# One transformer layer on one core: operand tiles alike modulo 512 bytes, border sums on VectorE, border loads ahead of the output product

## The chip, the cores and the metric

The kernel runs on 1 core of one Trainium2 chip. The metric is the device time of one execution in microseconds (us); lower is better. Each time is the median of several executions, with the lowest and the highest beside it. A profile is one execution of its own, with its own time.

## The reference

One layer over 2048 tokens of width 1024, with 256 context tokens, all in float32. The first half ends in the merge, the second is the feed-forward part:

```
y = sigmoid(ga) * (attn_o @ w_br_attn) + sigmoid(gb) * (gm_o @ w_br_gm)   # 512 -> 1024, twice
x = x + g1 * (y @ w_out)                                                  # 1024 -> 1024
h = rmsnorm(x, g) * (1 + scale) + shift
x = x + g2 * (square(relu(h @ w_ff1)) @ w_ff2)                            # 1024 -> 4096 -> 1024
```

Ahead of it stand the modulated norm, one input projection, attention (8 heads over 2 key heads, with rotary positions) and a gated branch over 128-token chunks.

## The kernel before

**Precision.** Each float32 operand of a large product is split into a high part (a rounding cast, mostly on ScalarE, lines L144, L970, L1139, L1174, L1180) and a low part (the difference, on VectorE or GpSimd, L148, L971, L1140, L1175, L1181). A product is then three matmuls (high x high, high x low, low x high): `mm3` (L176 to L178) in the merge, `product` (L1211 to L1213) in the feed-forward part. One matmul takes a 128x128 stationary tile and a 128x512 moving tile.

**Stages.** Projection, attention, merge (1479 to 1858 us in the trace), then feed-forward 1 and 2 for the first half of the tokens (to 2167 and 2480) and for the second (to 2800 and 3139). The merge takes four token blocks `b` of 512. In each, 8 steps `m` multiply the branch outputs (tiles `in`, moving) with the branch weights (`bw`, stationary), 24 matmuls a step; the gates `gt` multiply the sums, and the result is split into `y`. Then the output product follows: 4 row groups `tt` of two halves `n`, 24 matmuls each (`y` stationary, `wo` moving); VectorE multiplies each half with the gate (`jk`, L953) and a sum adds it to the residual `xt` (L955), which is stored (L957) and squared for the norm (L960). The branch weights are fetched and split anew in every block.

**Feed-forward 1** replaces eight block products by seven (a Strassen-like scheme over the two halves of the tokens and of the width). Group by group (`ff1_group`), the seven products of four 128-row steps each use sums of the normed input (`he` or `hl` tiles, high and low, moving) and of the weights (`f4`, `f2`, or `f8` for the first group, stationary). `f8` tiles hold loaded rows of x or weights, `f2` tiles sums and results in float32.

**The border.** What the first group needs is made during the output product of the last block (`b` = 3) by the generator `h_early`, which `merge` steps with `next(side)` after each half. For each of four inputs `kk` it loads x (`h_fetch`, L985, four transfers), scales it (`h_scaled`, L992), transposes it in four banks of four 128x128 blocks (`h_turn`, L182), moves them out through ScalarE (L999), and `combine` forms the sums; `halves` splits them. `h_last` forms one more sum; `h_rest`, stepped in the first group, splits what is left. `w1_fetch` loads the first group's weights (L1121), `w1_plain` and `w1_combine` make their parts and sums, and `w1_ops` the remaining parts, in steps.

**Order and memory.** Each engine runs its own queue in a fixed order, which a scheduler sets from the program's order and the dependencies; the method `order` keeps each tag's tiles in the order in which the program makes them. Tiles lie in pools on a left and a right side of the on-chip memory. The pool `edge` with the one tile `pd` is opened on the right first; so the right-hand tiles below it (`in`, `raw`, then `f8`, `f2`, `he`) start at addresses that its size shifts: 448 bytes past a multiple of 512 with `pd` of 8 floats. The left-hand tiles (`y`, `wo`, `bw`, `hl`, `f4`) start at multiples of 512.

```
self.open("edge", side="right")
self.nc.gpsimd.memset(self.sb("pd", [8]), 0.0)
self.open("pre", side="right")
```

Of the kernel before, what the change touches and what calls it, by code (L numbers as in the profile page):

```python
# [10 lines left out]
F32R = mybir.dt.float32r  # L11
I32 = mybir.dt.int32
AF = mybir.ActivationFunctionType
ALU = mybir.AluOpType
# [53 lines left out]
class Kern:  # L68
# [809 lines left out]
    def merge(self, first, start, last):  # L878
        nc = self.nc
        for _ in start:  # L880
            pass
        self.close("mid", "base")
        self.open("out")
        self.open("branch")
        steps = [(b, m) for b in range(NB) for m in range(KC)]
        it = iter(steps)
        q = []
        w_out = self.load_w_out()

        def fetch(lo_eng="pool"):  # L890
            s = next(it, None)
            if s is not None:
                q.append((self.br_weights(self.br_raw(s[1]), lo_eng), self.gate_in(*s)))

        inp = first
        early = [(s, self.br_raw(s[1])) for s in (next(it), next(it))]
        for s, raw in early:
            q.append((self.br_weights(raw, "dve"), self.gate_in(*s)))
        for b in range(NB):
            y = []  # L900
            for m in range(KC):
# [11 lines left out]
                nc.vector.tensor_tensor(out=gt["a"], in0=gt["a"], in1=gt["g"], op=ALU.add)  # L913
                yh, yl = self.sb("y", [TB], F32R), self.sb("y", [TB], F32R)
                self.split(gt["a"], yh, yl)
                y.append((yh, yl))
                if b == 0:
                    next(w_out, None)
                    if m == 2:
                        last.sums(self.sb("raw", [TB]))  # L920
                    if m == 4:
                        last.inverse()
            inp = {}
            if b + 1 < NB:
                side = self.br_inputs(b + 1, inp)
            else:
                self.close("branch", "pre")
                self.open("early", side="right")
                side = self.h_early()
            for tt in range(TT):  # L930
                tok = slice(tt * P, (tt + 1) * P)
                xt = self.sb("xt", [D])
                nc.sync.dma_start(xt, self.x_block(b)[tok, :])
                banks = [self.bank([512]) for _ in range(2)]

                def outer(n, ks):
                    cs = slice(n * 512, (n + 1) * 512)
                    for k in ks:
                        self.mm3(
                            banks[n], y[k][0][:, tok], y[k][1][:, tok], self.wo[k][0][:, cs],  # L940
                            self.wo[k][1][:, cs], k == 0, k == KC - 1,
                        )

                head = KC - 1 if tt == 0 else KC
                if tt == 0:
                    for n in range(2):
                        outer(n, range(head))
                for n in range(2):
                    cs = slice(n * 512, (n + 1) * 512)
# [3 lines left out]
                    nc.vector.tensor_tensor(out=part, in0=ps, in1=self.g1b[:, cs], op=ALU.mult)  # L953
                    eng = nc.vector if b + 1 < NB or tt + 1 == TT else nc.gpsimd
                    eng.tensor_tensor(out=xt[:, cs], in0=xt[:, cs], in1=part, op=ALU.add)  # L955
                    next(side, None)
                nc.sync.dma_start(self.x1_d[b][tok, :], xt)  # L957
# [75 lines left out]
    def h_early(self):  # L1033
        nc = self.nc
        add, sub = ALU.add, ALU.subtract
        self.h0 = h = [[None] * (KC // 2) for _ in range(7)]
        self.h0_src = src = {}

        def tt(out, in0, in1, op):
            nc.vector.tensor_tensor(out=out, in0=in0, in1=in1, op=op)  # L1040

        def ptt(out, in0, in1, op):
            nc.gpsimd.tensor_tensor(out=out, in0=in0, in1=in1, op=op)

        def done(kk, *ps):
            for p in ps:
                h[p][kk] = self.halves(kk, p, src[kk, p])

        def turn(kk, j):
            for i in range(2):  # L1050
                raw[kk, i, j] = self.h_turn(x[kk], kk, i, j)

        def combine(kk, tt):
# [12 lines left out]
        for kk in range(3):  # L1066
            x[kk] = self.h_fetch(0, kk)
        yield
        self.h_scaled(x[0], rb)
        turn(0, 0)  # L1070
        yield
        turn(0, 1)
        self.h_scaled(x[1], rb)
        combine(0, tt)
        done(0, 5)
        yield
        x[3] = self.h_fetch(0, 3)
        turn(1, 0)
        self.h_last(0, tt)
        done(0, 1, 6, 4)  # L1080
        yield
        turn(1, 1)
        self.h_scaled(x[2], rb)
        done(0, 3, 2)
        yield
        raw1 = self.w1_fetch(0)
        turn(2, 0)
        combine(1, tt)
        yield
        turn(2, 1)  # L1090
        self.h_scaled(x[3], rb)
        combine(2, ptt)
        yield
        turn(3, 0)
        turn(3, 1)
        combine(3, ptt)
        self.w1_first = self.w1_early(raw1)
        yield

    def h_last(self, kk, tt):  # L1100
        s2 = self.h0_src[kk, 2] = self.h0_src[kk, 5]
        tt(s2, self.h0_src[kk, 1], s2, ALU.subtract)

    def h_rest(self):
        h, src = self.h0, self.h0_src
        nc = self.nc

        def ptt(out, in0, in1, op):
            nc.gpsimd.tensor_tensor(out=out, in0=in0, in1=in1, op=op)

        for p in (5, 1, 6, 4, 3, 2):
            for kk in range(1, KC // 2):
                h[p][kk] = self.halves(kk, p, src[kk, p])
                if p == 5:
                    self.h_last(kk, ptt)
            yield

    def w1_fetch(self, g):
# [18 lines left out]
    def w1_plain(self, raw, hr, lr, out):  # L1137
# [8 lines left out]
    def w1_early(self, raw):  # L1146
        out = {}
        hl = self.sb("f8", [2, KC, P], F32R)
        self.w1_plain(raw, hl[:, 0], hl[:, 1], out)
        t = self.sb("f8", [2, 2, KC // 2, P])  # L1150
        self.w1_combine(raw, t[:, 0], t[:, 1])
        return out, raw, t[:, 0], t[:, 1]

    def w1_ops(self, g, out):
        if g == 0 and self.w1_first:
# [116 lines left out]
    def ff1(self, blk, h, extra):  # L1272
# [1 line left out]
        first = self.w1_ops(0, w[0])  # L1274
        rest = iter(()) if blk else self.h_rest()
        if blk == 0:
            for it in (first, rest, rest, first, first):
                next(it)
        for _ in first:
            pass  # L1280
        for g in range(NG):
            nxt = iter(())
            if g + 1 < NG:
# [2 lines left out]
            else:  # L1286
                self.ready = [self.ff2_chunk(blk, 0, 0)]
            more = extra(g)
            for _ in self.ff1_group(blk, g, w.pop(g), h):
                next(rest, None)  # L1290
                next(nxt, None)
                next(more, None)
            for _ in nxt:
# [111 lines left out]
    def build(self):  # L1405
# [312 lines left out]
```

## Time and profile before

| | |
|---|---|
| time, median of 3 (lowest to highest) | 3144.84 us (3142.81 to 3146.82) |
| profiled execution, its own time | 3140.78 us |
| its span in the trace | 3139.0 us |
| mean granted TensorE clock | 0.99 of full |
| busy: PE, DVE, ACT, POOL | 3066.5, 1947.1, 1352.2, 942.8 us |
| merge, border and first feed-forward group | 1479 to 1900 us of the span |

The profiled execution lies 4.06 us under the median, and 1.78 us of it lie outside the span. In the profile's rows PE is TensorE, PEld its weight loads, DVE VectorE, ACT ScalarE, POOL GpSimd and SP the engine whose queue issues the transfers. A row of a timeline gives the start and the duration in us, then engine, line, operation, output tile<-input tiles (`f` stands for f2, f4 and f8, `b` for a bank of the accumulation memory), and in brackets how long the engine had been idle and what ended that. Matmuls are pipelined: a record lasts longer than the distance to the next one's start.

### The profile page before, as it was taken

Reading aid. Unit: us, or ns where it says so; the run is one execution under the profiler, and the core shown is the slowest. Engines: PE = TensorE matmul, PEld = TensorE weight load, DVE = VectorE, ACT = ScalarE, POOL = GpSimd, SP = SyncE. Lnnn points to the kernel's source line nnn. Section 1 sums busy time; section 2 is a strip of 40 time slices with the busy share of each in tenths; the row PEclk is TensorE's granted clock in tenths of the full one; section 3 lists DMA queues with packets and bytes.
Section 4 is the critical chain, followed back from the end, with each engine's and each line's share of the span. In section 5 each row is a group of like instructions: output and inputs, shape, how many; then the busy total and the mean of one; then the engine's idle time right before and its main releaser. Section 6 shows DMA issues by size and latency. Waiting matters only on the chain.

```text
span 3139.0 us, 38055 instructions
## 1 busy us (share of the span) xinstructions
PE 3066.5 (98%) x13892; PEld 2305.2 (73%) x13892; DVE 1947.1 (62%) x2782; ACT 1352.2 (43%) x2058; POOL 942.8 (30%) x650
## 2 busy tenths in 40 slices
PE   8999999999999999999999999999999999999999
PEld 4888788877655555555777877888777788888777
DVE  4735666466677777667643478876654676654445
ACT  3353434333455555554322244444543344444433
POOL 1423323241688888887143230000000000000000
PEclk9999999999999999999999999999999999999999
DMA  6354655535100000003855548888576644445665
GB/s 202 110 181 118 203 156 179 185 98 174 38 14 4 21 8 18 11 8 93 270 159 162 158 138 313 307 298 279 196 256 205 212 146 152 153 144 194 207 214 201
DMA packets 332174, 485.42 MB, mean 155 GB/s; under 512 B 33969, under 2 KB 166321, under 8 KB 331986
## 3 DMA queue, kind: packets, MB, share of 16 engines
q1 hardware_dynamic: 324002, 478.38, 46.0%
q10 hardware_dynamic: 7984, 4.61, 0.5%
q8 instruction: 109, 1.79, 0.2%
q14 instruction: 79, 0.65, 0.1%
HBM read 348.56 MB, written 134.35 MB: 154 GB/s over the span
## 4 chain that ended last, share of the span: by engine, by line
PE 80%; DVE 7%; DMA 5%; POOL 3%; issue 2%; ACT 2%; SPq 0%; ACTq 0%; POOLq 0%; DVEq 0%
PE b L1212 12%; PE b L1213 12%; PE b L1211 11%; PE b L1610 8%; PE b L176 8%; PE b L178 8%; PE b L177 8%; PE b L1577 5%; PE b L1596 4%; PE b L1542 3%; PE b L182 2%; DMA bw<-in_w_br_gm 1%; DMA f<-w2o_d 1%; DMA w<-in_w_in 1%; POOL bw L148 1%
## 5 line engine op out<-in xcount | busy, mean ns | idle before, releaser
L1305 DVE TENSOR_TENSOR f<-f,f 128x1024 fp32r<-128x1024 f32 x224 | 273.1, 1224 | 267.4 <-ACT f L1304 264.2
L1553 DVE TENSOR_REDUCE ts<-b 128x1 f32<-128x512 f32 x512 | 314.8, 683 | 172.3 <-PE b L1542 172.3
L1304 ACT CAST f<-f 128x1024 fp32r<-128x1024 f32 x224 | 235.3, 1053 | 332.1 <-DMA f<-ao_d 289.6
L1212 PE MATMUL b<-f,f 128*128 128x512 f32 x896 | 350.9, 392 | 5.3 <-DVE f L1305 4.6
L1213 PE MATMUL b<-f,f 128*128 128x512 f32 x896 | 348.9, 389 | 0.0
L1626 POOL TENSOR_TENSOR ac<-ac,p 128x512 f32<-128x512 f32 x216 | 296.7, 1407 | 70.4 <-ACT p L1600 69.4
L1211 PE MATMUL b<-f,f 128*128 128x512 f32 x896 | 306.8, 392 | 11.0 <-ACT b L1347 4.9
L1600 ACT ACTIVATE p<-b 128x512 f32<-128x512 f32 x384 | 199.6, 614 | 158.0 <-PE b L1596 154.8
L148 POOL TENSOR_TENSOR w<-w,w 128x1024 fp32r<-128x1024 f32 x60 | 146.6, 2444 | 400.9 <-ACT w L144 166.7
L1626 POOL TENSOR_TENSOR ac<-ac,t 128x512 f32<-128x512 f32 x160 | 232.1, 1477 | 3.1 <-ACT t L1600 3.1
L1212 PE MATMUL b<-hl,f 128*128 128x512 f32 x576 | 226.6, 393 | 0.4 <-DVE hl L971 0.4
L1211 PE MATMUL b<-hl,f 128*128 128x512 f32 x576 | 225.8, 392 | 0.0
L1213 PE MATMUL b<-hl,f 128*128 128x512 f32 x576 | 224.5, 390 | 0.0
L144 ACT CAST w<-w 128x1024 fp32r<-128x1024 f32 x120 | 125.9, 1049 | 219.0 <-DMA w<-in_w_in 188.9
L176 PE MATMUL b<-t,w 128*128 128x512 f32 x512 | 204.9, 400 | 4.6 <-DVE t L590 4.2
L1211 PEld LDWEIGHTS b<-f,f 128*128 128x128 f32 x896 | 167.4, 188 | 52.1 <-ACT f L1304 8.2
L1212 PEld LDWEIGHTS b<-f,f 128*128 128x128 f32 x896 | 168.2, 188 | 46.6 <-DVE f L1305 12.2
L177 PE MATMUL b<-t,w 128*128 128x512 f32 x512 | 201.2, 393 | 0.0
L178 PE MATMUL b<-t,w 128*128 128x512 f32 x512 | 201.2, 393 | 0.0
L1577 PE MATMUL b<-t,t 128*128 128x512 f32 x576 | 198.1, 414 | 2.9 <-ACT p L1600 2.7
L178 PE MATMUL b<-w,t 128*128 128x512 f32 (+1 forms) x528 | 192.0, 364 | 2.6 <-POOL t L148 2.5
L1213 PEld LDWEIGHTS b<-f,f 128*128 128x128 f32 x896 | 168.2, 188 | 34.5
(230 smaller groups left out, 6518.5 us busy)
## 6 DMA issues: line engine op xcount, KB each, us to landing
w<-in_w_in SPq DMA_DIRECT2D x120, 512.0 KB
ao_d<-f SPq DMA_DIRECT2D x224, 256.0 KB
f<-ao_d SPq DMA_DIRECT2D x112, 512.0 KB
f<-w2o_d SPq DMA_DIRECT2D x112, 512.0 KB
f<-in_w_ff SPq DMA_DIRECT2D x48, 1024.0 KB
w2o_d<-f SPq DMA_DIRECT2D x112, 256.0 KB
md<-in_w_mod SPq DMA_DIRECT2D x32, 512.0 KB
f<-x_d SPq DMA_DIRECT2D x64, 256.0 KB
```

The source lines that it names most:

```text
L176: mm(ps, sh, mh, start=start, stop=False)
L177: mm(ps, sh, ml, start=False, stop=False)
L178: mm(ps, sl, mh, start=False, stop=stop)
L1211: mm(ps, wh, hh, start=start and k == 0, stop=False, skip_group_check=True)
L1212: mm(ps, wh, hl, start=False, stop=False, skip_group_check=True)
L1213: mm(ps, wl, hh, start=False, stop=k == len(w) - 1, skip_group_check=True)
L1304: nc.scalar.copy(h, f32(l))
L1305: nc.vector.tensor_tensor(out=l, in0=f32(l), in1=f32(h), op=ALU.subtract)
L1553: nc.vector.tensor_reduce(out=self.mx[:, t, h, c : c + 1], in_=ps[h], axis=AX.X, op=ALU.max)
L1577: self.nc.tensor.matmul(self.pts[j][h], k.KA[c][self.kv][:, ks], self.qa[h], start=True, stop=False, skip_group_check=True,)
L1610: nc.tensor.matmul(self.o[h * HD : (h + 1) * HD, :], k.V[c][:, i, self.kv * HD : (self.kv + 1) * HD], pt[h], start=j == 0, stop=j == NKT - 1,)
L1626: nc.gpsimd.tensor_tensor(out=self.acc[e][:, h], in0=old[:, h], in1=pt[h], op=ALU.add)
```

## The change

1. `pd` has 120 floats instead of 8 (480 bytes instead of 32), which shifts all right-hand tiles by 448 bytes, to multiples of 512.
2. Fifteen sums at the border go from GpSimd to VectorE: six into `xt`, six of `combine` (for `kk` = 2 and 3) and three of `h_last`.
3. `h_early` is cut anew. Its first step (the loads for `kk` = 0 to 2) is taken ahead of the output product; each later step transposes a whole input (16 blocks); the first group's weights are loaded a step earlier; and the last step of `w1_ops` (the split for product 2) goes behind the fourth product of the first group instead of ahead of the first.

```diff
@@ merge
                 side = self.h_early()
+                next(side)
...
-                    eng = nc.vector if b + 1 < NB or tt + 1 == TT else nc.gpsimd
-                    eng.tensor_tensor(out=xt[:, cs], in0=xt[:, cs], in1=part, op=ALU.add)
+                    nc.vector.tensor_tensor(out=xt[:, cs], in0=xt[:, cs], in1=part, op=ALU.add)
                     next(side, None)
@@ h_early
-        def turn(kk, j):
-            for i in range(2):
-                raw[kk, i, j] = self.h_turn(x[kk], kk, i, j)
+        def turn(kk):
+            self.h_scaled(x[kk], rb)
+            for j in range(2):
+                for i in range(2):
+                    raw[kk, i, j] = self.h_turn(x[kk], kk, i, j)
...
         yield
-        self.h_scaled(x[0], rb)
-        turn(0, 0)
-        yield
-        turn(0, 1)
-        self.h_scaled(x[1], rb)
-        combine(0, tt)
+        turn(0)
+        yield
+        combine(0)
         done(0, 5)
-        yield
         x[3] = self.h_fetch(0, 3)
-        turn(1, 0)
-        self.h_last(0, tt)
-        done(0, 1, 6, 4)
-        yield
-        turn(1, 1)
-        self.h_scaled(x[2], rb)
-        done(0, 3, 2)
-        yield
+        yield
+        turn(1)
         raw1 = self.w1_fetch(0)
-        turn(2, 0)
-        combine(1, tt)
-        yield
-        turn(2, 1)
-        self.h_scaled(x[3], rb)
-        combine(2, ptt)
-        yield
-        turn(3, 0)
-        turn(3, 1)
-        combine(3, ptt)
-        self.w1_first = self.w1_early(raw1)
-        yield
+        self.h_last(0)
+        done(0, 1, 6)
+        yield
+        done(0, 4, 3, 2)
+        combine(1)
+        yield
+        turn(2)
+        combine(2)
+        yield
+        turn(3)
+        out, hl = {}, self.sb("f8", [2, KC, P], F32R)
+        self.w1_plain(raw1, hl[:, 0], hl[:, 1], out)
+        yield
+        combine(3)
+        t = self.sb("f8", [2, 2, KC // 2, P])
+        self.w1_combine(raw1, t[:, 0], t[:, 1])
+        self.w1_first = out, raw1, t[:, 0], t[:, 1]
+        yield
@@ h_rest
-                    self.h_last(kk, ptt)
+                    self.h_last(kk)
@@ ff1
-            for it in (first, rest, rest, first, first):
+            for it in (first, rest, rest, first):
                 next(it)
-        for _ in first:
-            pass
+        else:
+            for _ in first:
+                pass
...
-            for _ in self.ff1_group(blk, g, w.pop(g), h):
+            for n, _ in enumerate(self.ff1_group(blk, g, w.pop(g), h)):
                 next(rest, None)
+                if n == 3:
+                    next(first, None)
@@ build
-        self.nc.gpsimd.memset(self.sb("pd", [8]), 0.0)
+        self.nc.gpsimd.memset(self.sb("pd", [120]), 0.0)
```

The queues change only at the border. First, TensorE's queue before, at the end of the output product (`wo`, `y`), where the fourth input's transposes (L182, `ident`; x4 is four blocks in one bank) stand between it and the first product of feed-forward 1 (L1211):

```order
L176 MATMUL b_15978<-wo_13560,y_15628 128x512
L177 MATMUL b_15978<-wo_13561,y_15628 128x512
L178 MATMUL b_15978<-wo_13560,y_15629 128x512
L182 MATMUL b_16056<-ident,f_3566_15832 128x128 x4
L182 MATMUL b_16063<-ident,f_3566_15832 128x128 x4
L182 MATMUL b_16070<-ident,f_3566_15832 128x128 x4
L182 MATMUL b_16077<-ident,f_3566_15832 128x128 x4
L1211 MATMUL b_16145<-he_15796,f_3623_16092 128x512
L1212 MATMUL b_16145<-he_15797,f_3623_16092 128x512
```

Now, TensorE's queue has the same four rows of transposes ahead of the last row group of the output product:

```order
L176 MATMUL b_15902<-wo_13560,y_15628 128x512
L177 MATMUL b_15902<-wo_13561,y_15628 128x512
L178 MATMUL b_15902<-wo_13560,y_15629 128x512
L182 MATMUL b_15995<-ident,f_3560_15770 128x128 x4
L182 MATMUL b_16002<-ident,f_3560_15770 128x128 x4
L182 MATMUL b_16009<-ident,f_3560_15770 128x128 x4
L182 MATMUL b_16016<-ident,f_3560_15770 128x128 x4
L176 MATMUL b_16031<-wo_13164,y_15317 128x512
L177 MATMUL b_16031<-wo_13165,y_15317 128x512
```

Behind them 48 output matmuls follow, and then the first product, whose line is now L1195 (L1211 to L1213 became L1195 to L1197).

Second, ScalarE's queue at the start of feed-forward 1, before: the split of product 2's weights (L1180), the weight casts (L1174), the casts of the inputs, and last the copy of the first product's bank (L1230):

```order
L960 ACTIVATE jk_3625_16100,ss2_78<-xt_3600_15975 128x1024
L1180 CAST f2_3642_16141<-f8_3591_15948 128x512
L1174 CAST f4_3626_16106<-f8_3624_16095 128x1024
L970 CAST hl_3628_16110<-f2_3568_15842 128x512
L1174 CAST f4_3640_16137<-f8_3624_16095 128x1024
L970 CAST hl_3630_16115<-f2_3593_15955 128x512
L970 CAST hl_3632_16120<-f2_3613_16061 128x512
L970 CAST hl_3634_16125<-f2_3583_15903 128x512
L970 CAST hl_3636_16129<-f2_3605_16011 128x512
L970 CAST hl_3638_16133<-f2_3617_16075 128x512
L1230 COPY f2_3646_16159<-b_3644_16145 128x512
```

Now the same place of ScalarE's queue (L1214 is the copy, L1158 the weight cast):

```order
L960 ACTIVATE jk_3625_16100,ss2_78<-xt_3616_16029 128x1024
L1214 COPY f2_3644_16155<-b_3642_16141 128x512
L1158 CAST f4_3626_16106<-f8_3623_16068 128x1024
L970 CAST hl_3628_16110<-f2_3567_15815 128x512
L1158 CAST f4_3640_16137<-f8_3623_16068 128x1024
L970 CAST hl_3630_16115<-f2_3595_15936 128x512
L970 CAST hl_3632_16120<-f2_3607_16000 128x512
L970 CAST hl_3634_16125<-f2_3571_15829 128x512
L970 CAST hl_3636_16129<-f2_3599_15950 128x512
L970 CAST hl_3638_16133<-f2_3611_16014 128x512
```

The copy moved from behind the casts to ahead of them, and the split L1180 went from this place to a later one.

Third, VectorE's queue at the same place, now (L1159 is the low part of the weights, before L1175; L1097 is `h_last`, before L1109 on GpSimd):

```order
L955 TENSOR_TENSOR xt_16029<-xt_16029,jk_16096 128x512
L1159 TENSOR_TENSOR f_3627_16107<-f_3623_16068,f_3626_16106 128x1024
L971 TENSOR_TENSOR hl_16111<-f_3567_15815,hl_16110 128x512
L1159 TENSOR_TENSOR f_3641_16138<-f_3623_16068,f_3640_16137 128x1024
L1097 TENSOR_TENSOR f_3567_15815<-f_3571_15829,f_3567_15815 128x512
L971 TENSOR_TENSOR hl_16116<-f_3595_15936,hl_16115 128x512
L971 TENSOR_TENSOR hl_16121<-f_3607_16000,hl_16120 128x512
L1097 TENSOR_TENSOR f_3595_15936<-f_3599_15950,f_3595_15936 128x512
L1097 TENSOR_TENSOR f_3607_16000<-f_3611_16014,f_3607_16000 128x512
L971 TENSOR_TENSOR hl_16126<-f_3571_15829,hl_16125 128x512
```

The three rows of L1097 are new in this queue; the sums of `combine` (L1040) and into `xt` (L955) stand ahead of these rows. GpSimd's queue ends with the last split of `y` in the merge.

More of the change, by code (lines that the diff above doesn't have):

```diff
@@ L1040, in tt @@
             nc.vector.tensor_tensor(out=out, in0=in0, in1=in1, op=op)
-        def ptt(out, in0, in1, op):
-            nc.gpsimd.tensor_tensor(out=out, in0=in0, in1=in1, op=op)
         def done(kk, *ps):
@@ L1047, in done, with combine @@
                 h[p][kk] = self.halves(kk, p, src[kk, p])
-        def turn(kk, j):
-            for i in range(2):
-                raw[kk, i, j] = self.h_turn(x[kk], kk, i, j)
-        def combine(kk, tt):
+        def turn(kk):
[3 more added lines that the diff above has]
+                    raw[kk, i, j] = self.h_turn(x[kk], kk, i, j)
+        def combine(kk):
             r = {(i, j): raw[kk, i, j] for i in range(2) for j in range(2)}
@@ L1068, in h_early, with h_last @@
         yield
-        self.h_scaled(x[0], rb)
-        turn(0, 0)
+        turn(0)
         yield
-        turn(0, 1)
-        self.h_scaled(x[1], rb)
-        combine(0, tt)
+        combine(0)
         done(0, 5)
+        x[3] = self.h_fetch(0, 3)
         yield
-        x[3] = self.h_fetch(0, 3)
-        turn(1, 0)
-        self.h_last(0, tt)
-        done(0, 1, 6, 4)
+        turn(1)
+        raw1 = self.w1_fetch(0)
+        self.h_last(0)
+        done(0, 1, 6)
         yield
-        turn(1, 1)
-        self.h_scaled(x[2], rb)
-        done(0, 3, 2)
+        done(0, 4, 3, 2)
+        combine(1)
         yield
-        raw1 = self.w1_fetch(0)
-        turn(2, 0)
-        combine(1, tt)
+        turn(2)
+        combine(2)
         yield
-        turn(2, 1)
-        self.h_scaled(x[3], rb)
-        combine(2, ptt)
+        turn(3)
+        out, hl = {}, self.sb("f8", [2, KC, P], F32R)
+        self.w1_plain(raw1, hl[:, 0], hl[:, 1], out)
         yield
-        turn(3, 0)
-        turn(3, 1)
-        combine(3, ptt)
-        self.w1_first = self.w1_early(raw1)
+        combine(3)
+        t = self.sb("f8", [2, 2, KC // 2, P])
+        self.w1_combine(raw1, t[:, 0], t[:, 1])
+        self.w1_first = out, raw1, t[:, 0], t[:, 1]
         yield
-    def h_last(self, kk, tt):
+    def h_last(self, kk):
         s2 = self.h0_src[kk, 2] = self.h0_src[kk, 5]
-        tt(s2, self.h0_src[kk, 1], s2, ALU.subtract)
+        self.nc.vector.tensor_tensor(
+            out=s2, in0=self.h0_src[kk, 1], in1=s2, op=ALU.subtract
+        )
     def h_rest(self):
         h, src = self.h0, self.h0_src
-        nc = self.nc
-        def ptt(out, in0, in1, op):
-            nc.gpsimd.tensor_tensor(out=out, in0=in0, in1=in1, op=op)
         for p in (5, 1, 6, 4, 3, 2):
@@ L1144, in w1_plain @@
         out[1] = [(hr[:, H + k, :], lr[:, H + k, :]) for k in range(H)]
[L1146 to L1152, printed above, removed]
     def w1_ops(self, g, out):
```

## Prediction

> **What bounds the kernel now.** I read the busy times first, then the chain, then stretches of one stage at a time.
>
> ```profile
> span 3139.0 us, 38055 instructions
> PE 3066.5 (98%) x13892; PEld 2305.2 (73%) x13892; DVE 1947.1 (62%) x2782; ACT 1352.2 (43%) x2058; POOL 942.8 (30%) x650
> PE 80%; DVE 7%; DMA 5%; POOL 3%; issue 2%; ACT 2%; SPq 0%; ACTq 0%; POOLq 0%; DVEq 0%
> ```
>
> TensorE carries 80% of the chain, so two things can move the end: the pitch of its matmuls, and its pauses. The windows on PE alone show the pitch (us, busy time, number, granted clock, DMA share, GB/s); in each PE is busy throughout at full clock.
>
> ```profile
> core 0: us, PE busy (x), PEclk, DMA share, GB/s
> 1534.00:1564.00 30.00, 30.00 (x134) 1.00 0.77 257
> 1770.00:1800.00 30.00, 30.00 (x130) 1.00 0.50 149
> 1900.00:2160.00 260.00, 260.00 (x1130) 1.00 0.89 306
> 2920.00:2950.00 30.00, 30.00 (x134) 1.00 0.57 191
> ```
>
> A matmul reaches 0.39 us past its start, so a 30 us window holds starts over 30.39 us. The first (output product, `wo` and `y`) gives 30.39/134 = 226.8 ns, the second (branch product, `in` and `bw`) 30.39/130 = 233.8 ns, the third (feed-forward 1, mostly `he` or `hl` against `f`) 260.39/1130 = 230.4 ns, the last (feed-forward 2) 226.8 ns. All are 128x512 float32 products. By tile, the third window splits:
>
> ```profile
> 1900.00:2160.00 260.00, 105.64 (x399) 74.76 (x400) 0.00 (x0) 0.00 (x0) 1.00 0.89 306
> 1900.00:2160.00 260.00, 180.37 (x731) 136.64 (x729) 0.00 (x0) 0.00 (x0) 1.00 0.89 306
> 2565.95 0.39 PE L1211 MATMUL b<-he,f 128*128 128x512 f32 x1
> 2569.44 0.39 PE L1211 MATMUL b<-hl,f 128*128 128x512 f32 x1
> ```
>
> The first row is `he` (399 matmuls), the second `hl` (731). The last two bracket an unbroken run of 15 `he` products: 3.49/15 = 232.7 ns. Then `hl` costs (260.39 - 399 x 0.2327)/731 = 229.2 ns. So the operands that start 448 bytes past a multiple of 512 (`in`, `he`) stream at 233 ns against a weight tile at 0, and those at 0 against 0 (`wo`, `y`, `hl`) at 227 to 229. A busy PE hides this, since overlapping records fill the window either way.
>
> **The change, part by part.**
>
> *Alignment.* The larger `pd` shifts every right-hand tile by 448 bytes, so `in`, `raw`, `f8`, `f2` and `he` come to 0 modulo 512, as the left-hand tiles are. The counts, from the groups by tile (duration min/median/max, first and last start):
>
> ```profile
> L1211 PE MATMUL b<-he,f x320: 389/394/796, 1857.9 to 2814.9; 128*128 128x512 f32 x160
> L176 PE MATMUL b<-in,bw x256: 392/394/628, 1479.2 to 1806.6; 128*128 128x512 f32 x128
> ```
>
> The other two lines of each product have as many: 960 `he` and 768 `in` matmuls. For `he` I take the pitch of `hl`, its neighbour in the same groups: 3.5 ns x 960 = 3.4 us; with feed-forward 2's pitch it would be 5.9 ns x 960 = 5.7 us. The lower end is zero (a rival). Feed-forward 1 runs without pauses from 1900 on, so the gain reaches the end. The shifted `f2` weights have no pitch of their own in a row; I cost them at nothing, within 0.5 us.
>
> In the merge only matmuls on the path count. The chain by line for 1479 to 1858, and for the stretch in which the third token block's branch products run:
>
> ```profile
> by line: PE b L178 24.4%; PE b L176 24.2%; PE b L177 23.9%; DMA bw<-in_w_br_gm 11.4%; POOL bw L148 7.5%; issue 2.2%; ACT bw L144 2.2%; PE b L182 1.5%; POOL y L148 0.7%; DVE gt L913 0.4%; DVE in L148 0.4%; PE b L1652 0.3%; POOLq L148 0.2%; D
> by line: POOL bw L148 36.7%; DMA bw<-in_w_br_gm 35.8%; issue 8.8%; ACT bw L144 7.2%; POOL y L148 4.1%; PE b L178 3.6%; PE b L176 1.9%; PE b L177 1.9%; POOLq L148 1.1%; ACTq L144 0.1%
> ```
>
> L176 to L178 hold 72.5% of 379 us = 275 us. The output product's 768 matmuls take 768 x 0.2268 = 174 us of that, which leaves 101 us, or 430 of the 768 branch matmuls at 0.2338. The second row (1688 to 1722) says why the others don't count: weights are fetched and split there, and a faster PE only waits longer. 430 x 7.0 ns = 3.0 us; with the `he`/`hl` difference, 430 x 3.5 = 1.5. I take 2.3. Both ends: nothing, and 768 x 7.0 = 5.4.
>
> [...]
>
> *Border: adds and order.* Fifteen additions leave GpSimd for VectorE (six into `xt`, six in `combine`, three in `h_last`). VectorE does such an operation in 0.60 to 0.69 us; the rows show what it costs beside GpSimd.
>
> ```profile
> 1852.13 4.88 POOL L1043 TENSOR_TENSOR f<-f,f 128x512 f32<-128x512 f32 x3 [5.85 <-ACT f L999]
> 1866.53 2.20 POOL L1109 TENSOR_TENSOR f<-f,f 128x512 f32<-128x512 f32 x1 [1.90 <-DVE hl L971]
> 1869.36 3.35 POOL L1109 TENSOR_TENSOR f<-f,f 128x512 f32<-128x512 f32 x2 [0.63 <-DVE hl L971]
> 1860.21 1.62 DVE L971 TENSOR_TENSOR he<-f,he 128x512 fp32r<-128x512 f32 x1
> 1867.50 5.75 DVE L971 TENSOR_TENSOR hl<-f,hl 128x512 fp32r<-128x512 f32 x4
> 1873.17 0.68 DVE L1181 TENSOR_TENSOR f<-f,f 128x512 fp32r<-128x512 f32 x1
> 1850.10 0.69 DVE L953 TENSOR_TENSOR jk<-b,g 128x512 f32<-128x512 f32 x1 [1.41 <-PE b L178]
> ```
>
> Twelve of the fifteen go ahead of the first feed-forward product: 12 x 0.6 = 7.2 us of new VectorE work, hidden in its idle time of 1.41 us before the last row and like gaps from 1815 to 1858. Without that cover they cost 7.2 us. The other three, 3 x 0.6 = 1.8 us, fall in the first group, where VectorE has no room:
>
> ```profile
> 1868.00:1900.00 32.00, 28.75 (x117) 22.01 (x117) 31.96 (x44) 18.13 (x30) 4.08 (x3) 0.97 0.79 272
> 1857.91 0.48 PE L1211 MATMUL b<-he,f 128*128 128x512 f32 x1
> 1861.88 0.50 PE L1212 MATMUL b<-he,f 128*128 128x512 f32 x1 [1.15 <-DVE he L971]
> 1864.64 0.80 PE L1211 MATMUL b<-he,f 128*128 128x512 f32 x1 [2.03 <-ACT f L1174]
> 1866.92 0.63 PE L1211 MATMUL b<-he,f 128*128 128x512 f32 x1
> 1867.35 0.63 PE L1212 MATMUL b<-hl,f 128*128 128x512 f32 x1
> 1874.00 0.50 PE L1211 MATMUL b<-he,f 128*128 128x512 f32 x1 [2.34 <-ACT f L1230]
> 1888.88 0.50 PE L1213 MATMUL b<-he,f 128*128 128x512 f32 x1 [0.31 <-DVE f L1175]
> ```
>
> VectorE is busy 31.96 of 32 us, yet four subtractions of 0.6 took 5.75, beside GpSimd. PE waits 1.15, 2.03 and 2.34 us; after the second its pitch is 0.43 us instead of 0.23 (1866.92 to 1867.35) for about a dozen matmuls: 12 x 0.2 = 2.4 us at half clock. The last row is the 88th feed-forward matmul, 30.97 us after the first; 87 at 230.4 ns need 20.0, so the border now costs 11 us.
>
> After the change the fourth input's 16 transposes stand ahead of 48 output matmuls (48 x 0.2268 = 10.9 us), so its `he` is ready at the start: the first product loses nothing (gain: 1.15 us of wait). The copy of its result (0.59) now stands in ACT's queue ahead of the cast L1158 (before: L1174) of the second weights, and VectorE's subtraction L1159 behind that:
>
> ```profile
> 1863.54 1.04 ACT L1174 CAST f<-f 128x1024 fp32r<-128x1024 f32 x1 [1.81 <-DVE f L1135]
> 1864.62 1.23 DVE L1175 TENSOR_TENSOR f<-f,f 128x1024 fp32r<-128x1024 f32 x1 [1.11 <-ACT f L1174]
> 1873.36 0.59 ACT L1230 COPY f<-b 128x512 f32<-128x512 f32 x1 [4.70 <-DVE hl L971]
> ```
>
> 0.59 + 1.04 + 1.23 = 2.9 us pass between the first product's end and the second's last weights. Nine matmuls of the third product and then those of the second that need only the high part run in that time, so I see waits of about 0.8, 0.3 and 0.7 us. From there VectorE paces PE, with each low part 0.6 (an `hl`) or 1.2 us (weights) after the last, three adds between them: eight waits of 0.2 to 1.7, together some 6 us. Sum: 20.0 + 1.8 + 6 = 27.8, against 30.97: 3.2 us. Of these 2.4 are the half clock; it followed a wait of 2.03, and none of my waits is that long. They could chain, so I take 2.8; the ends are +4 and, with half clock back and 1.8 us of adds uncovered, 4.2 - 3.2 = 1.0 lost.
>
> *Moved loads.* The fourth input's four issues and the weights' one stand earlier in SP's queue, each past one store of `x1`.
>
> ```profile
> 1799.85 10.02 SPq L985 DMA_DIRECT2D f<-x_d  x12
> 1826.89 2.02 SPq L985 DMA_DIRECT2D f<-x_d  x4
> 1834.53 0.33 SPq L957 DMA_DIRECT2D x_d<-xt  x1
> 1838.29 0.37 SPq L1121 DMA_DIRECT2D f<-in_w_ff  x1
> ```
>
> SP is idle from 1828.9 to 1834.5 and nothing that PE waits for comes from those stores: nothing, unless the weights came late, and they only come earlier. The 12 early loads stood ahead of the output product already.
>
> *Sum:* 3.4 + 2.3 + 2.8 = 8.5 us. The profiled execution, 3140.78 us (its span and 1.78 outside), becomes 3132.3. The median of three lies 4.06 above it, so 3136.3.
>
> **The rivals.**
>
> 1. *Alignment pays nothing.* The 7 ns come from something else that sets these stages apart, such as which side of memory a tile is on. For it: `hl` at 0 is still 2.4 ns over feed-forward 2. Against: `in` and `he`, in stages with different DMA load (0.50 and 0.89), show the same 233. [...] Only the border's 2.8 is left: 3142.0.
> 2. *Waits take the gains back.* In the merge a PE 7 ns faster waits for the weights as in the 1688 to 1722 row, and VectorE's queue gives the border nothing. Only `he` pays: 3144.8 - 3.4 = 3141.4. DMA at 0.89 in feed-forward 1 works the same way.
> 3. *All of it pays.* 5.7 + 5.4 + 4 = 15.1: 3129.7.
> 4. *Slower: VectorE's queue at the border.* The 15 adds find no idle time, because the transposes' results and the squares in ACT's queue come later than I see; each then costs its 0.69 us on the path, 10.4 in all, and the product that waits for the last of them waits over 2 us, so that the half clock comes a second time (2.4). Against it: the idle stretches of VectorE before 1858. It decides at a wait of 2.0 us at a product behind the first. 10.4 + 2.4 - 5.7 of alignment = 7.1 lost: 3151.9.
>
> **How the numbers follow.** The forecast 0.50, its own range a gain of 5 to 12 us (3132.8 to 3139.8); rival 1 0.17; rival 2 0.14; rival 3 0.10; rival 4 0.09. A measurement here can tell 0.2% = 6.3 us from no change. The forecast falls beyond 6.3 in four fifths of its cases (0.40), rival 3 always (0.10), rival 2 in 0.04: faster 0.54 and I add 0.04 for rival 1 where the border alone gives much. Slower is two thirds of rival 4: 0.06 (the rest of it, with less than the full price, is no change). The rest, 0.36, is no change. Leaving out the far ends of rivals 3 and 4, the range is 3130 to 3144.
>
> **What would show it.** Right: the stretch of `in` holds 133 or 134 matmuls in 30 us; 260 us of feed-forward 1 hold 1134 or more; no GpSimd addition after the merge's last split; no half-clock pitch after the first feed-forward product; its 88th matmul about 28 us after it. Wrong: 130 matmuls in `in`'s stretch (rival 1), longer waits for `bw` and `y` at an unchanged merge (rival 2), or a wait over 2 us on ACT's cast in the first group (rival 4).

## The result and the profile after

| | before | after |
|---|---|---|
| time, median of 4 (lowest to highest) | 3145.60 us (3142.81 to 3146.82) | 3122.80 us (3120.28 to 3126.11) |
| profiled execution: span | 3139.0 us | 3119.3 us |

The ratio of after to before is 0.9929, with a 95% interval from 0.9912 to 0.9947: 22 us faster, between 17 and 28. The forecast was 3136.3 us, with a range from 3130 to 3144; the measured time lies under it. One execution of a kernel below, e6, took 7220.89 us at a granted clock of 0.40 and is left out of that kernel's time.

The page of after, in the same rows as before's, and the windows on PE alone (us, busy time, number of matmuls, granted clock, DMA share, GB/s):

```profile
span 3119.3 us, 38046 instructions
PE 3045.5 (98%) x13892; PEld 2299.1 (74%) x13892; DVE 1937.7 (62%) x2797; ACT 1352.0 (43%) x2058; POOL 917.5 (29%) x635
PE 79%; DVE 7%; DMA 6%; POOL 3%; ACT 2%; issue 2%; SPq 0%; ACTq 0%; DVEq 0%; POOLq 0%
...
1534.00:1564.00 30.00, 30.00 (x134) 1.00 0.64 217
1770.00:1800.00 30.00, 30.00 (x134) 1.00 0.58 180
1900.00:2140.00 240.00, 240.00 (x1059) 1.00 0.89 314
2490.00:2760.00 270.00, 270.00 (x1192) 1.00 0.41 145
```

The bound is the same engine; PE is busy throughout in each window, as before. Only the counts tell what changed. The second row's 30 us, nearly all of them branch products, hold 134 matmuls instead of 130: 30.39/134 = 226.8 ns. The first 240 us of feed-forward 1 hold 1059, 227.0 ns each. The same windows of before:

```profile
1900.00:2140.00 240.00, 240.00 (x1043) 1.00 0.89 306
2490.00:2760.00 270.00, 270.00 (x1174) 1.00 0.43 147
```

1059 against 1043 is 16 matmuls, 3.6 us in 240; that is more than `he` alone could give, as the tile rows of after show (first `he`, then `hl`, each with its number of matmuls):

```profile
1900.00:2140.00 240.00, 97.16 (x375) 69.78 (x373) 0.00 (x0) 0.00 (x0) 1.00 0.89 314
1900.00:2140.00 240.00, 167.45 (x684) 128.50 (x685) 0.00 (x0) 0.00 (x0) 1.00 0.89 314
```

(375 + 684) x 227.0 ns fill the window: if `hl` had stayed at 229.2, its 684 alone would leave 240.39 - 156.8 = 83.6 us, or 223 ns for each `he`, less than the pitch of any stage in these traces. Both went to 227.

The starts of the second half of the tokens, averaged by place in the product, say where `hl` lost. In five of the seven products of a group three `he` matmuls are followed by nine `hl`, with `f4` weights; neither `hl` nor `f4` moved. Before, the first five `hl` took 226, 236, 228, 233 and 231 ns and only those from the sixth on 227; after, all take 226 to 227. So the slow pitch of `he` ran on into its neighbours. Product 2, the last of a group, is another case: its weights are `f2` tiles, which the larger `pd` does move, from 448 to 0, so that its `hl` matmuls, at 0, stood 448 bytes off their own weights. The distance from its first row to that of the next group (two rows of before, then two of after) was 2.78 us and is 2.72:

```profile
2563.17 0.39 PE L1211 MATMUL b<-he,f 128*128 128x512 f32 x1
2565.95 0.39 PE L1211 MATMUL b<-he,f 128*128 128x512 f32 x1
2548.38 0.39 PE L1195 MATMUL b<-he,f 128*128 128x512 f32 x1
2551.10 0.39 PE L1195 MATMUL b<-he,f 128*128 128x512 f32 x1
```

Of some 327 ns lost in a group of 84 matmuls, the `he` matmuls themselves made 172, the `hl` matmuls behind them 99, and product 2 made 56.

The border, PE's waits summed for 1845 to 1905 (engine, line, what it waited for: us in total, times, longest):

```profile
PE b L1196 <- DVE hl L971: 2.1, 3, 1.1
PE b L1197 <- DVE f L1159: 1.9, 2, 1.4
PE b L1195 <- ACT f L1214: 0.7, 1, 0.7
PE b L1197 <- DVE f L1132: 0.2, 1, 0.2
```

```profile
1849.13 0.39 PE L1195 MATMUL b<-he,f 128*128 128x512 f32 x1
...
1876.87 0.50 PE L1197 MATMUL b<-he,f 128*128 128x512 f32 x1 [1.37 <-DVE f L1159]
...
1877.98 0.63 PE L1197 MATMUL b<-hl,f 128*128 128x512 f32 x1
1878.41 0.63 PE L1195 MATMUL b<-hl,f 128*128 128x512 f32 x1
```

The waits are the ones forecast: ACT's copy (0.7), the second weights (0.5 of the 1.9), then VectorE's low parts. The 88th matmul comes 27.74 us after the first (forecast 27.8, before 30.97). The half clock is back at another place, behind the last wait: pitch 0.43 us from about 1877.6 on, at a granted clock of 0.50 from 1877.50 to 1880.00, some 1.6 us lost. From the 88th to the 121st product it takes 9.23 us here, and 7.60 in the trace of e5, which has no half clock there.

Of the 19.7 us between the two spans, 6.8 lie ahead of the merge, 1.9 in it, 3.2 between the first and the 88th feed-forward product, 1.7 in the rest of feed-forward 1's first half and 4.7 in its second half; the rest lies elsewhere. The first branch product starts at 1479.2 us before and at 1472.3 after:

```profile
L176 PE MATMUL b<-in,bw x256: 387/389/500, 1472.3 to 1797.9; 128*128 128x512 f32 x128
```

Nothing is changed in the queues ahead of that point. Whether the addresses did that had to be tested.

### The profile page after: what moved, and what is told of

Its sections match the earlier page's. It is cut to its first block, busy times and chain, and to the rows that moved or that the text cites. A ratio compares the mean times of both kernels' runs of the same rounds, so it can differ in the third digit from the quotient of the medians.

```text
span 3119.3 us, 38046 instructions
## 1 busy us (share of the span) xinstructions
PE 3045.5 (98%) x13892; PEld 2299.1 (74%) x13892; DVE 1937.7 (62%) x2797; ACT 1352.0 (43%) x2058; POOL 917.5 (29%) x635
## 4 chain that ended last, share of the span: by engine, by line
PE 79%; DVE 7%; DMA 6%; POOL 3%; ACT 2%; issue 2%; SPq 0%; ACTq 0%; DVEq 0%; POOLq 0%
PE b L1196 12%; PE b L1197 12%; PE b L1195 11%; PE b L1597 8%; PE b L176 7%; PE b L178 7%; PE b L177 7%; PE b L1564 5%; PE b L1583 4%; PE b L1529 3%; PE b L182 2%; DMA bw<-in_w_br_gm 1%; DMA w<-in_w_in 1%; DVE f L1292 1%; DMA f<-ao_d 1%
## 5 line engine op out<-in xcount | busy, mean ns | idle before, releaser
L1197 PE MATMUL b<-f,f 128*128 128x512 f32 x896 | 348.9, 389 | 0.0
L1195 PE MATMUL b<-f,f 128*128 128x512 f32 x896 | 306.6, 391 | 10.2 <-ACT b L1334 4.5
L1195 PE MATMUL b<-hl,f 128*128 128x512 f32 x576 | 224.6, 390 | 0.0
L1197 PE MATMUL b<-hl,f 128*128 128x512 f32 x576 | 224.3, 390 | 0.0
L1195 PEld LDWEIGHTS b<-f,f 128*128 128x128 f32 x896 | 167.5, 188 | 50.8 <-ACT f L1291 7.0
L1197 PEld LDWEIGHTS b<-f,f 128*128 128x128 f32 x896 | 168.2, 188 | 34.4
```

The lines of the kernel that those rows point to most:

```text
L1195: mm(ps, wh, hh, start=start and k == 0, stop=False, skip_group_check=True)
L1197: mm(ps, wl, hh, start=False, stop=k == len(w) - 1, skip_group_check=True)
```

## The experiments

Theories: (A) alignment, the border and a chance difference ahead of the merge add up; (B) what is gained ahead of the merge belongs to the change; (C) order and sums bring most of it. Each timed kernel was run beside the kernel before on the same chip; ratios are to that, with a 95% interval.

**e1, no alignment** (all else changed):

```diff
-        self.nc.gpsimd.memset(self.sb("pd", [120]), 0.0)
+        self.nc.gpsimd.memset(self.sb("pd", [8]), 0.0)
```

> The changed kernel with pd at 8 floats again: sums and order as changed, right-hand tiles back at 448 modulo 512. Theory A (alignment, border and chance ahead of the merge add up): 260 us of feed-forward 1 hold about 1130 matmuls again, 30 us of the in/bw stretch 130; the 88th feed-forward product stays about 28 us after the first; time 3142 us (3139 to 3145), 3 us under before. The merge's start in the trace falls anywhere from 1472 to 1481 us. Theory B (the 6.8 us gained ahead of the merge belong to the addresses): the merge starts at 1478 or later. Theory C (order and sums bring most of the 22.8 us): 3130 or less.

Measured: 3133.63 us against 3138.94, ratio 0.9986 (0.9977 to 0.9994): 4.4 us faster (2 to 7). That is theory A's 3 us in size; the time itself lies under the expected range because the kernel before was faster too in this comparison than in the first. Feed-forward 1 is back at the pitch of before; the 88th product comes 27.30 us after the first; the merge starts at 1479.7.

```profile
1900.00:2140.00 240.00, 239.99 (x1040) 1.00 0.88 308
2490.00:2760.00 270.00, 270.00 (x1174) 1.00 0.43 149
```

**e2, alignment alone** (`pd` of 120 floats in the kernel before):

```diff
-        self.nc.gpsimd.memset(self.sb("pd", [8]), 0.0)
+        self.nc.gpsimd.memset(self.sb("pd", [120]), 0.0)
```

> The kernel before with pd at 120 floats: alignment alone. Theory A: feed-forward 1 at 227 ns a matmul for he and hl alike, 2688 x 3.5 ns = 9.4 us less, the merge 2 to 3 less, border as before (88th product some 30.5 us after the first, half clock kept): 3133.5 us (3130 to 3137). Theory B: another 6.8 us less, 3127, and the merge starts at 1473. Theory C: 3142 or more.

Measured: 3124.23 us, ratio 0.9955 (0.9943 to 0.9967): 14.1 us faster (10 to 18). Theory A expected 11 us less than before and theory B 18, and the interval holds both; the border and the merge's start tell more. The border stays as it was (30.97 us to the 88th product).

```profile
1900.00:2140.00 240.00, 240.00 (x1060) 1.00 0.87 312
2490.00:2760.00 270.00, 270.00 (x1192) 1.00 0.41 144
```

The two parts add to 18.5 us. Theory C falls. The merge started at 1478.0 us here, not near theory B's 1473, so with the new addresses too it can start as late as with the old.

**e3, the border's sums alone** (order and `pd` as before):

```diff
-                    eng = nc.vector if b + 1 < NB or tt + 1 == TT else nc.gpsimd
-                    eng.tensor_tensor(out=xt[:, cs], in0=xt[:, cs], in1=part, op=ALU.add)
+                    nc.vector.tensor_tensor(out=xt[:, cs], in0=xt[:, cs], in1=part, op=ALU.add)
...
-            nc.gpsimd.tensor_tensor(out=out, in0=in0, in1=in1, op=op)
+            nc.vector.tensor_tensor(out=out, in0=in0, in1=in1, op=op)
```

> The kernel before with the fifteen border sums on VectorE and nothing else changed (the order of loads and transposes and pd of 8 as before). If the contention with GpSimd is the border's loss, the 88th feed-forward product comes 28 us after the first and the time is 3142; if the order of the transposes is, the sums add to VectorE's queue and it comes 31 to 33 us after: 3145 to 3148.

Measured: 3136.31 us, ratio 0.9991 (0.9981 to 1.0002), 2.6 us less in the median, which this can't tell from none. But in the trace the 88th product comes 27.95 us after the first, 3.0 sooner, although half clock follows the wait of 1.5 us as it did before. No GpSimd instruction runs beside VectorE any more; VectorE's subtractions take 0.6 to 0.7 us each where four took 5.75 before, and the long wait of 2.3 us for ACT's copy is gone (three waits of PE, then a row of VectorE).

```profile
PE b L1210 <- ACT f L1173: 1.5, 1, 1.5
PE b L1211 <- DVE he L970: 0.6, 1, 0.6
PE b L1211 <- DVE hl L970: 0.4, 1, 0.4
1876.92 1.28 DVE L970 TENSOR_TENSOR hl<-f,hl 128x512 fp32r<-128x512 f32 x2
```

**e10, the new order alone, at the new addresses** (the fifteen sums on GpSimd again in the changed kernel; one execution):

```diff
-                    nc.vector.tensor_tensor(out=xt[:, cs], in0=xt[:, cs], in1=part, op=ALU.add)
+                    eng = nc.vector if b + 1 < NB or tt + 1 == TT else nc.gpsimd
+                    eng.tensor_tensor(out=xt[:, cs], in0=xt[:, cs], in1=part, op=ALU.add)
...
+            tt = ptt if kk > 1 else vtt
...
-        self.nc.vector.tensor_tensor(
+        eng = self.nc.gpsimd if kk else self.nc.vector
+        eng.tensor_tensor(
```

> The changed kernel with its new order and its addresses, but the fifteen sums on GpSimd as before. If the sums bring the border's 3 us, the 88th feed-forward product comes about 31 us after the first, or later; if the new order brings it, about 27.5.

Measured: 3126.89 us; the 88th product after 29.26 us, between the two: the order alone brings 1.7 us, the sums alone 3.0, both together 3.2 to 3.7. They overlap, and neither theory's number was met. With the sums on GpSimd the slow subtractions are back:

```profile
1865.18 5.79 DVE L972 TENSOR_TENSOR hl<-f,hl 128x512 fp32r<-128x512 f32 x4
```

What the order takes away is the wait of 1.5 to 2.0 us for the cast of the second weights: it stands in all four traces with the old order (before, e2, e3 and e6), each time with half clock behind it (a pitch of 0.43 us in before and e3), and in none with the new.

**e5, the changed kernel again**, beside e6, a kernel with alignment and sums in the old order:

> The changed kernel once more, unchanged, beside e6 on one chip. Theory A (alignment 12 to 14 us, border 3 to 4, the rest of the 22.8 us chance in the merge's start): 16 to 19 us under before. Theory B (the part ahead of the merge belongs to the change): 21 us or more under before, and the merge starts near 1472 again. A half clock behind the wait of 1.4 us at the 88th product comes in some executions and not in others.

> The kernel before with pd at 120 floats and the fifteen sums on VectorE, but with the loads, transposes and splits in the order of before. If the new order of h_early brings something, this is 1 us or more slower than the changed kernel; if the sums bring all of the border's gain, the two are equal within their scatter, 16 to 19 us under before, and the 121st feed-forward product comes 33.5 to 35.7 us after the first (changed kernel: 36.97 with a half clock).

Measured: the changed kernel 3122.89 us, ratio 0.9957 (0.9941 to 0.9973), 13.5 us faster (8 to 19); the other 3121.7 in four executions, ratio 0.9949 (0.9934 to 0.9963). They are equal within their scatter: on top of the sums, the new order brings nothing that the times can show; in the traces the 88th product comes 0.7 us sooner with it (27.27 against 27.94). Nor do the times show the border's gain on top of alignment, which alone gave 14.1 us in e2; it is seen in e1's time and in the traces. The changed kernel took the same time as in the first comparison (3122.8); it was the kernel before that read 3145.6 there, and 3138.3 here. The merge starts at 1479.4 in this trace of the changed kernel, 7 us later than in the first. Over all traces of this case it starts at 1472.3 to 1481.8 with distances that are multiples of 256 bytes (eight traces, mean 1478.7) and at 1477.1 to 1485.4 with others (six, mean 1480.1). Theory B isn't borne out; what a small mean difference there is, these traces can't tell from scatter.

The half clock behind the 88th product didn't come in e5's trace, after the same wait:

```profile
1881.17 0.50 PE L1197 MATMUL b<-he,f 128*128 128x512 f32 x1 [1.37 <-DVE f L1159]
1881.50 0.40 PE L1195 MATMUL b<-hl,f 128*128 128x512 f32 x1
1881.73 0.39 PE L1196 MATMUL b<-hl,f 128*128 128x512 f32 x1
```

**e4, e7, e11, e8: which addresses are alike?** One execution each: `pd` of 56, 88 and 104 floats in the changed kernel (right-hand tiles at 256, 128 and 64 modulo 512), and one with all feed-forward tiles at 448:

```diff
-    "late": {"hl": 36, "f4": 12},
+    "late": {"lp": 1, "hl": 36, "f4": 12},
...
         self.open("late")
+        self.nc.gpsimd.memset(self.sb("lp", [112]), 0.0)
...
-        self.nc.gpsimd.memset(self.sb("pd", [120]), 0.0)
+        self.nc.gpsimd.memset(self.sb("pd", [8]), 0.0)
```

> The changed kernel with pd at 56 floats: right-hand tiles at 256 modulo 512 instead of 0. If equality modulo 512 is what counts, he runs at 230 ns or more against 227, and the matmuls after it are slowed for a few places too; if it is equality modulo 256 or less, he and hl stay at 226.8 and 240 us of feed-forward 1 hold 1059 matmuls.

> The changed kernel with right-hand tiles at 128 modulo 512 (pd of 88 floats). If equality modulo 256 is needed, he runs above 230 ns and 240 us of feed-forward 1 hold about 1043 matmuls; if equality modulo 128 is enough (448 is 64 modulo 128), they hold 1059.

> The changed kernel with right-hand tiles at 64 modulo 512 (pd of 104 floats), so at the other sign of 448. If only distances that are multiples of 256 are fast, 240 us of feed-forward 1 hold about 1043 matmuls and a branch product runs at 233 ns; if small distances are cheaper, they hold 1050 or more.

> The changed kernel with pd at 8 floats and a pad tile of 112 floats first in the left pool of the feed-forward part: he, hl, f8, f4 and f2 all at 448 modulo 512, in and bw at 448 and 0 as before. If the distance between moving and stationary tile counts, 240 us of feed-forward 1 hold 1059 matmuls and feed-forward 2 runs at 227 ns, the merge at 233; if each tile's own address counts, feed-forward 1 and 2 both run at 233 ns, and feed-forward 2's 30 us hold 130.

Measured: 3123.45, 3136.32, 3143.77 and 3127.26 us. The same window of each, in that order:

```profile
1900.00:2140.00 240.00, 240.00 (x1056) 1.00 0.88 313
1900.00:2140.00 240.00, 240.00 (x1040) 1.00 0.88 307
1900.00:2140.00 240.00, 240.00 (x1037) 1.00 0.87 307
1900.00:2140.00 240.00, 239.76 (x1055) 1.00 0.90 313
```

At a distance of 256 bytes the pitch is the short one (1056); at 128 and 64 it is the long one, as at 448. The branch product differs: at 128 its block takes 44.79 us, as at 448, but at 64 only 43.96, or 229 ns a matmul, where 233 was expected. With all tiles at 448 the feed-forward part is fast and the branch product, still 448 against 0, stays slow: 108 matmuls in the 25 us from 1770, where e4 has 112. So of the addresses tried it is the distance between moving and stationary tile that counts, and 256 (1056 matmuls) is about as good as 0 (1059); "alike modulo 512" is more than is needed. No run here names the mechanism.

**e9 and e12, what is left of the merge.** In the traces so far the output products of blocks 2 and 3 took 47.7 to 51.6 us, where 192 matmuls at 226.8 ns need 43.6. VectorE shows one reason (before, behind block 2's branch products):

```profile
1623.50 3.02 DVE L148 TENSOR_TENSOR in<-raw,in 128x512 fp32r<-128x512 f32 x2 [9.71 <-ACT in L144]
1626.44 0.68 DVE L910 SCALAR_TENSOR_TENSOR gt<-gt,b 128x512 f32<-128x512 f32 x1
1627.04 0.68 DVE L148 TENSOR_TENSOR in<-raw,in 128x512 fp32r<-128x512 f32 x1
...
1631.50 0.68 DVE L913 TENSOR_TENSOR gt<-gt,gt 128x512 f32<-128x512 f32 x1
```

The low parts of the next block's inputs stand ahead of the last step's gate products (L910) in its queue and wait 9.71 us for ScalarE's cast. Holding them back, for blocks 2 to 4:

```diff
                 h, l = self.sb("in", [TB], F32R), self.sb("in", [TB], F32R)
+                at = self.here()
                 self.split(raw, h, l, lo_eng="dve")
+                if b:
+                    self.fixed.append(range(at, self.here()))
```

> The changed kernel, with VectorE's low parts of the next token block's inputs (in, L148) held behind the program's earlier VectorE work, so that they no longer stand ahead of the last step's gate products (L910). If that place in the queue makes the waits for y at the start of the output products of blocks 2 and 3 (VectorE idle 7 to 10 us there while L910 could run), these two output products take 43.6 to 46 us instead of 50, and the time is 8 to 13 us under the changed kernel's: 3110 to 3115. If GpSimd's queue of weight splits or the weights' transfers make the waits, they stay near 50 us each and the time is 3121 to 3125. A third way: the next block's branch products wait instead for the inputs held back, and half of the gain is lost.

Measured: 3120.51 us, ratio 0.9941 (0.9926 to 0.9956). The output products of blocks 2 and 3 fell to 47.9 us each, a third to a half of what was expected; the time can't be told from the changed kernel's. VectorE's gate products now run at once (L913, sum L916), and the next queue shows:

```profile
1621.69 0.69 DVE L916 TENSOR_TENSOR gt<-gt,gt 128x512 f32<-128x512 f32 x1
1625.92 0.61 ACT L144 CAST y<-gt 128x512 fp32r<-128x512 f32 x1
1629.63 0.62 ACT L144 CAST bw<-bw 128x512 fp32r<-128x512 f32 x1 [3.10 <-DMA bw<-in_w_br_gm]
1631.70 0.62 ACT L144 CAST bw<-bw 128x512 fp32r<-128x512 f32 x1 [1.45 <-POOL bw L148]
1632.23 0.61 ACT L144 CAST y<-gt 128x512 fp32r<-128x512 f32 x1
```

`y` is ready to be cast at 1622.4 and is cast at 1632.2 (the last row), behind weight casts that wait for transfers; that is 9.8 us, more than the 3.5 that the next expectation names. So both parts of `y` went to VectorE, on top of the edit before:

```diff
-                self.split(gt["a"], yh, yl)
+                self.split(gt["a"], yh, yl, *(("dve", "dve") if b else ("act", "pool")))
```

> The kernel of e9 with both parts of y (cast and low part) on VectorE for the second to the fourth token block, so that y stands in neither ScalarE's nor GpSimd's queue behind weight splits that wait for transfers. If those queues make what is left of the waits (in e9 1.6, 0.8 and 1.1 us of PE's idle time at the second block's output product, with ScalarE's cast of y 3.5 us behind VectorE's last gate product), the output products of blocks 2 and 3 take 43.6 to 44.5 us instead of 47.9 and the time falls by 7 to 9 us, to 3112 to 3114. If the weights' supply is the bound, the wait comes back at the next block's branch products and the time stays at 3118 to 3121.

Measured: 3106.90 us (3105.80 to 3109.15), ratio 0.9905 (0.9889 to 0.9922): 30 us faster than the kernel before (24 to 35), and the best kernel of this case. That is 13.6 us under e9, more than the 7 to 9 expected; the merge accounts for 10.7 of it in the traces (372.4 to 361.7 us). The first three output products take 43.5 us each, and 90 us across block 2 are without a pause:

```profile
1570.00:1660.00 90.00, 90.00 (x399) 1.00 0.57 181
```

## Why the prediction was wrong

*The direction, and the effect of alignment*: right. Equal addresses bring 226.8 ns; rival 1 (the address does nothing) is refuted by the kernels that differ in `pd` alone: the 240 us of feed-forward 1 hold 1043 matmuls before and 1060 in e2, 1040 in e1 and 1059 after.

*The step that failed first: the pitch of `he` was compared with that of `hl`, as if `hl` were untouched.* The term "3.5 ns x 960 = 3.4 us" measured 9.2: from the 88th product to the end of feed-forward 1's first half 290.0 to 290.5 us with distances off a multiple of 256 (four traces, mean 290.2) and 285.3 to 287.0 with multiples (the five without a half clock there, e8 left out, mean 286.0), 4.2 less; in the second half 309.9 against 304.8, 5.0 less. Added up by place in the product, some 5.2 us of this are `he`'s own, near the prediction's other figure of 5.7, and some 2.7 the tail of `he` in `hl`. The rest, some 1.5, is product 2 with its `f2` weights, the term that was put "at nothing, within 0.5 us"; its `hl` matmuls were not 0 against 0, as the prediction took all of `hl` to be. The row that showed it was in the first table: 2688 matmuls at 230.4 against feed-forward 2's 226.8 is 9.7 us. I had split the stage's loss by tile and then taken the smaller part as the floor.

*The second: "only matmuls on the path count", 430 of 768.* The chain put the stretch from 1688 to 1722 down to the weights' supply, but PE ran without a pause in the branch products, and the wait behind them is for `y`, which e12 took away with the same weights to fetch. So a faster branch product is not lost in a wait for weights. Block 2's branch products start and end at

```profile
1572.97 0.39 PE L176 MATMUL b<-in,bw 128*128 128x512 f32 x1
1617.77 0.39 PE L176 MATMUL b<-wo,y 128*128 128x512 f32 x1
1565.05 0.39 PE L176 MATMUL b<-in,bw 128*128 128x512 f32 x1
1608.57 0.39 PE L176 MATMUL b<-wo,y 128*128 128x512 f32 x1
```

(the first two before, the others after): 44.80 against 43.52 us, 1.3 less, and the same in blocks 3 and 4; with as much in block 1, where waits hide it, 5 in all, where I took 2.3. Block 2's output product took the same at both kinds of distance: 50.2 us in the mean of five traces off a multiple of 256, 50.3 in six with multiples; block 3's took 49.6 and 50.6, within a scatter of 47.7 to 51.6. (e9 and e12, which change these waits, and e11 with its other pitch are left out here.) The merge as a whole took 379.7 and 375.4 us: 4.3 less. PE's waits for `y` sum to 7.9 and 7.7 us in the mean, so on the whole the gain wasn't taken back, and rival 2 falls too. In the first pair it mostly was, 5.8 us of waits before and 9.2 after, which left 1.9 us in the merge; that pair alone would have spoken for rival 2.

*The border: right in size* (2.8 forecast; 3.2 in the pair of traces, 3.7 in the next), and the waits came at the rows named. Its account of the half clock failed: I let it hang on a wait of 2.0 us. Behind the same wait of 1.37 to 1.39 us at the same instruction it came in four of nine traces (the first of the changed kernel, e9, e11 and e12) and stayed away in five (e1, e4, e5, e7 and e8). Where it came it took back half of the border's gain.

*The moved loads and rival 4*: no wait over 2 us came in the first group, and nothing waited for the moved loads.

*What neither covers*: 9.2 + 4.3 + 3.2 to 3.7 = 17, against 22 (17 to 28) in the first comparison and 13.5 (8 to 19) in the repeat. The first interval just holds it, the second does too. Taken from the same 3145.6 us, 17 gives 3128.6, under the range's 3130: the terms alone carry the miss, and the other 6 us are luck of the first comparison. Rival 3, with 15.1, was nearest and had a chance of 0.10. The kernel before scatters from 3129.05 to 3146.82 us over this case; 6.8 us of the first pair's 19.7 lay ahead of the merge, where a wait in the projection and a half clock at the end of attention (granted 0.64 from 1454 to 1458 us before, 1.00 after) were missing in that one execution of the changed kernel. What makes that scatter stays open.

## What to carry to other kernels

Count matmuls in a window in which the engine never pauses, and compare stages that do the same operation: the best of them (here 226.8 ns) is the floor, not the neighbour. Where moving and stationary operands come from pools with different offsets, try other distances between them; a pad tile sets one. Here 0 and 256 bytes gave 227 to 228 ns a matmul, and 64, 128 and 448 gave 229 to 234. A wait that looks like one for supplies may be one for an answer: look at what stands ahead in the queue of the engine that has to give it. Moving that (e9 and e12) brought some 16 us here, about as much as the whole change.

## What the runs showed of the hardware

In block 2's branch products 192 matmuls, 128x512 in float32, took 43.52 us with moving and stationary tile at a distance of 0 (after), or 226.7 ns each; 44.80 us at 448 (before) and 44.79 at 128 (e7), or 233.3; and 43.96 at 64 (e11), or 229. The first 240 us of feed-forward 1 held 1059 matmuls at 0 (after) and 1056 at 256 (e4), against 1043 at 448 (before), 1040 at 128 (e7) and 1037 at 64 (e11). In before the slow pitch lasted for some five matmuls into products whose own distance was 0 (226 to 236 ns in the mean, 227 from the sixth on). What makes the difference no run here shows.

Four subtractions on VectorE took 5.75 us beside GpSimd additions (before; 5.79 in e10), and without them 0.6 to 0.7 each (e3).

The half clock was a granted clock of 0.50 and a pitch of 0.43 us instead of 0.23 (before, 1864.6 to 1869.9; after, 1877.50 to 1880.00). A wait of 1.37 us at one and the same instruction was followed by it in the trace of after and not in those of e1, e4 and e5, so the length of the wait alone didn't decide it here. Nor did a longer one always bring it: in before it followed the wait of 2.03 us, and behind the wait of 2.34 us (1874.00) the clock was 1.00. What decides it no run here shows.
